# The start of a two-layer diffusion backbone: the first norm's squares and shift modulation on TensorE, the context's scale modulation on VectorE

## The chip, the cores and the metric

The kernel runs on one core of a Trainium2 chip. The metric is the device time of one execution in microseconds. Of several runs the median is taken. One further execution was taken by the hardware profiler; its times are those of the profile. The engines are called as the profile calls them: PE is TensorE, DVE is VectorE, ACT is ScalarE, POOL is GpSimd, SP is the engine that issues the DMA transfers.

## What is computed

The model has 512 latent tokens and 256 context tokens of width 1024, and two layers. Each sub-layer first normalises its input and modulates it. The start of the program, which is where the change lies, is this part of the reference:

```python
m_lat = jnp.moveaxis((jax.nn.silu(c) @ mod_w[l] + mod_b[l]).reshape(b, N_MOD, 1, D_MODEL), 1, 0)
m_ctx = (jax.nn.silu(c_ctx) @ mod_w[l] + mod_b[l]).reshape(N_MOD, 1, 1, D_MODEL)

def rmsnorm(x, g):
    xf = x.astype(jnp.float32)
    y = xf * lax.rsqrt(jnp.mean(xf * xf, axis=-1, keepdims=True) + EPS)
    return (y * g.astype(jnp.float32)).astype(x.dtype)

def modulate(h, g, shift, scale):
    return rmsnorm(h, g) * (1 + scale) + shift

def ffn_sublayer(h, m, j, g_pre, g_post, w13, w2):
    a = modulate(h, g_pre, m[3 * j], m[3 * j + 1])
    return h + FFN_RES * m[3 * j + 2] * rmsnorm(swiglu(a, w13, w2), g_post)
```

So before the first matrix product can run, the mean square of every token is needed, and two of the nine modulation vectors: the shift and the scale, each a product of the activated conditioning vector (one for latent, one for context tokens) with a 1024 x 1024 block of `mod_w`. The rest of the two layers (attention in the first, a state-space scan in the second, four feed-forward sub-layers, and the other modulation vectors) is not touched by the change.

## The kernel before

Activations are held with the feature on the partition: `h` has eight k tiles of 128 features, each 128 x 512 (latent) or 128 x 256 (context). Every large product keeps float32 accuracy with three matmuls: weights and activations are split in a high and a low part, and `mm3` (L861 to L863) issues high x high, high weight x low activation, low weight x high activation. The high part is made on ACT, the low part on DVE.

`start` prepares the first feed-forward sub-layer and returns `feed`, which is called once for each k tile, here called steps 0 to 7. The order is written out by hand; no planner places this work. Each engine runs its own instructions in the order of the program, so what stands first in `start` and `feed` stands first in its engine's queue.

* The squares of the latent tokens: ACT squares each k tile (`sq_acc`, L892 and L898), DVE adds seven of them into a sum (L899), and `rstd_a` lets PE sum over partitions by four products with a column of ones (L873). DVE adds the epsilon (L875), POOL takes the power -1/2 (L876), and `rstd_b` spreads the result over the partitions on PE (L883); that spread tile, in PSUM, is called R below.
* The modulation: the block of `mod_w` is read transposed, 16 tiles of 128 outputs x 1024 inputs (half a megabyte each): `m0d8` to `m0d15` for the scale, `m0d0` to `m0d7` for the shift, in a ring of nine buffers. For latent tokens DVE makes one dot per tile (`dot`, L651: product with the broadcast conditioning vector `cb` and sum). For context tokens POOL multiplies the tile in place (`prod`, L523) and ACT sums it (`close`, L516); four such tiles may be pending. `gains` (L505, L506) and `shifts` (L511) add the bias.
* The normalised activations: DVE makes `tmp` (L552), ACT its high part `ahi` with the shift as bias (L555), DVE the low part `alo` (L556).
* The weights of the first three rows of the feed-forward part are split by `high` (L496, ACT) and `low` (L500, DVE), two per row (gate and up).

Between the steps PE runs the matmuls that have become possible: the first row from step 0, the second from step 1, the third from step 4, at most two k tiles of a row at a time until the last step. That makes 6, 18, 12, 12, 24, 24, 24 and 24 matmuls in steps 0 to 7, 144 in all, called the first block here. Step 0 also issues all later transfers on SP, in order: the modulation tiles, the weights of rows 1 and 2, then the context tokens; step 7 issues the first background tiles (`mw`) and weights, and squares the context tokens. After the block the outputs of the three rows leave PSUM (L1056 on ACT, L1059 on DVE) and the context's chain begins. The remaining modulation tiles are worked off by DVE during the later matmuls, for both kinds of tokens.

Of the kernel before, what the change touches and what calls it, by code (L numbers as in the profile page):

```python
# [10 lines left out]
F32 = mybir.dt.float32  # L11
F32R = mybir.dt.float32r
AF = mybir.ActivationFunctionType
ALU = mybir.AluOpType
PSUM = bass.MemoryType.PSUM

P = 128
D = 1024
KT = D // P
NL = 512  # L20
# [5 lines left out]
LAT, CTX = 0, 1  # L26
# [21 lines left out]
LZP = 0.3  # L48
SALT = None
TRACE = None  # L50
CTXD = ()
HI = (1, 1, 2, 3)
FROM = (0, 1, 4)
CATCH = 2
# [14 lines left out]
class Graph:  # L69
# [4 lines left out]
    LAT = 0.15  # L74
# [337 lines left out]
class Model:  # L412
# [40 lines left out]
    def start(self, a, l=0, s=0):  # L453


        nc, tc, io = self.nc, self.tc, self.io
        m0 = tc.alloc_tile_pool(name="m0", bufs=1)
        self.cb = [self.modp.tile([P, D], F32, name=f"cb{v}") for v in (LAT, CTX)]
        cf = self.pp.tile([P, 2, 2, 8], F32, name=f"coef{l}_{s}")
        self.coef[l, s] = cf  # L460
        self.bg_done.update(((0, 0), (0, 1)))
        mod, bias, held, wd, prods, ws = self.modc[0], self.vec("mod_b0"), [], {}, [], {}
        box = [{}, {}]

        def load_c(v):
            nc.sync.dma_start(out=self.cb[v], in_=io[("c", "c_ctx")[v]].partition_broadcast(P))

        def silu(v):
            nc.scalar.activation(self.cb[v], self.cb[v], AF.Silu)

        def load(m):
            for t in (8 + m, m):
                wd[t] = m0.tile([P, D], F32, tag="wd", name=f"m0d{t}", bufs=9)
                nc.sync.dma_start(out=wd[t], in_=io["mod_wT"][0, t])

        def weights(r):

            if r == 2:
                n = [x.rearrange("p k t -> p (k t)") for x in self.new_a(CTX)]
            for up in (0, 1):  # L480
                if r == 1:
                    raw = m0.tile([P, SLOT], F32, name=f"m0raw{up}")
                    hi, lo = [m0.tile([P, SLOT], F32R, name=f"m0{x}{up}") for x in ("whi", "wlo")]
                else:
                    raw = self.wp.tile([P, SLOT], F32, tag="raw", name=f"raw{self.uid()}", bufs=2)
                    if r == 0:
                        hi, lo = [self.wp.tile([P, SLOT], F32R, tag=x, name=f"{x}{self.uid()}", bufs=3)
                                  for x in ("whi", "wlo")]
                    else:
                        hi, lo = [x[:, up * SLOT:(up + 1) * SLOT] for x in n]  # L490
                nc.sync.dma_start(out=raw, in_=io["w13"][0, 0, r, up])
                ws[r, up] = raw, hi, lo

        def high(r, up):
            raw, hi, lo = ws[r, up]
            nc.scalar.activation(hi, raw, AF.Copy)  # L496

        def low(r, up):
            raw, hi, lo = ws[r, up]
            nc.vector.tensor_tensor(lo, raw, hi.bitcast(F32), op=ALU.subtract)  # L500

        def gains(v, m, n=1):

            sh, sc = slice(m, m + n), slice(8 + m, 8 + m + n)
            nc.vector.tensor_tensor(mod[:, v, sc], mod[:, v, sc], bias[:, sc], op=ALU.add)  # L505
            nc.vector.scalar_tensor_tensor(cf[:, v, 0, sh], mod[:, v, sc], 1.0, self.vec("npre00")[:, sh],  # L506
                                           op0=ALU.add, op1=ALU.mult)

        def shifts(v, m, n=1):
            sh = slice(m, m + n)  # L510
            nc.vector.tensor_tensor(mod[:, v, sh], mod[:, v, sh], bias[:, sh], op=ALU.add)  # L511

        def close(n):
            while len(prods) > n:
                t = prods.pop(0)
                nc.scalar.activation(wd[t], wd[t], AF.Copy, accum_out=mod[:, CTX, t:t + 1])  # L516

        def prod(t):

            if t in CTXD:  # L520
                self.mod_dot(wd[t], 0, t, CTX)
            else:
                nc.gpsimd.tensor_tensor(wd[t], wd[t], self.cb[CTX], op=ALU.mult)  # L523
                prods.append(t)

        def dot(t):
            self.mod_dot(wd[t], 0, t, LAT)

        self.load_h(LAT, 2)
        load_c(LAT)  # L530
        load(0)
        for t, name in ((self.vecs, "vecs"), (self.ident, "ident")):
            nc.sync.dma_start(out=t, in_=io[name])
        weights(0)
        load_c(CTX)
        load(1)
        for m in range(KT):
            self.sq_acc(self.h[LAT][:, m], NL, m, box[LAT], nc.vector)
        silu(LAT)
        dot(8)  # L540
        self.rstd_a(box[LAT]["S"], NL, box[LAT])
        dot(0)
        gains(LAT, 0)
        shifts(LAT, 0)
        self.rstd_b(NL, box[LAT])
        high(0, 0)
        a[LAT]["hi"], a[LAT]["lo"] = self.new_a(LAT)

        def pre(k):

            t = self.tmp()
            nc.vector.scalar_tensor_tensor(t, self.h[LAT][:, k], cf[:, LAT, 0, k:k + 1], box[LAT]["R"],  # L552
                                           op0=ALU.mult, op1=ALU.mult)
            hi, lo, sh = a[LAT]["hi"][:, k], a[LAT]["lo"][:, k], mod[:, LAT, k:k + 1]
            nc.scalar.activation(hi, t, AF.Identity, bias=sh)  # L555
            return lambda: nc.vector.scalar_tensor_tensor(lo, t, sh, hi.bitcast(F32), op0=ALU.add, op1=ALU.subtract)  # L556

        def feed(k):
            if k == 0:
                load(2)  # L560
                weights(1)
                for m in range(3, KT):
                    load(m)
                    if m == W2:
                        weights(2)
                self.load_h(CTX)
            rest = pre(k)
            if k == 0:
                high(0, 1)
                silu(CTX)  # L570
                for t in (8, 0):
                    prod(t)
                low(0, 0)
            elif k + 1 < KT:
                dot(9 + k)
            rest()
            if k == 0:
                low(0, 1)
                dot(9)
            if k + 1 < KT:  # L580
                gains(LAT, k + 1)
                dot(1 + k)
                shifts(LAT, k + 1)
                for t in (9 + k, 1 + k):
                    prod(t)
            for i in range(4):
                if HI[i] == k:
                    high(1 + i // 2, i % 2)
                    low(1 + i // 2, i % 2)
            close(4)  # L590
            if k == KT - 1:
                self.mw_load()
                self.prime()
                for m in range(KT):
                    self.sq_acc(self.h[CTX][:, m], NCX, m, box[CTX], nc.vector)

        def done():
            self.ahead = 4

        self.ahead, self.quiet = 1, True  # L600
        tag = ("chain", l, -1, CTX, 0)
        first = 144 * NL / 2400.0
        self.seq.defer(first + 0.1, tag, lambda: (gains(CTX, 0, KT), shifts(CTX, 0, KT)))
        self.chain_pre(CTX, 0, NCX, l, s, box[CTX], first + T0C, tag, a[CTX])
        return feed, lambda: (close(0), m0.release()), done, ws

    def vec(self, name):
# [257 lines left out]
    def rstd_a(self, S, n, box, inv=1.0 / D):  # L865

        nc = self.nc
        nb = n // P
        ps = self.sbank()
        for b in range(nb):  # L870
            at = [b * P, 256 + b * P] if n <= 256 and inv == 1.0 / D else [b * P]
            for c in at:
                nc.tensor.matmul(ps[:, b:b + 1], S[:, c:c + P], self.ones[:, 0:1], start=c == at[0], stop=c == at[-1])  # L873
        r = self.tp.tile([P, 8], F32, tag="r", name=f"r{self.uid()}", bufs=4)
        nc.vector.tensor_scalar(r[:, :nb], ps[:, :nb], inv, EPS, op0=ALU.mult, op1=ALU.add)  # L875
        nc.gpsimd.tensor_tensor(r[:, :nb], r[:, :nb], self.mhalf[:, :nb], op=ALU.pow)  # L876
        box["r"] = r
# [1914 lines left out]
def layout(inputs):  # L2792

    a = {k: np.asarray(v) for k, v in inputs.items()}
    c = np.ascontiguousarray
    o = {}
# [11 lines left out]
    for l in range(2):  # L2808
        put(f"mod_b{l}", col(a["mod_b"][l]))
        for s in range(3):  # L2810
# [3 lines left out]
    put("kvn", col(a["mla_kv_norm"][0]))  # L2814
    put("sink", np.broadcast_to(a["swa_sink"][0][None, :], (P, 8)))
    o["vecs"] = vecs
    o["w13"] = c(a["ffn_w13"].reshape(2, 2, KT, P, 2, NFF, P).transpose(0, 1, 5, 4, 3, 2, 6)
                 .reshape(2, 2, NFF, 2, P, KT * P))
    o["w2"] = c(a["ffn_w2"].reshape(2, 2, NFF, P, KT, P).transpose(0, 1, 4, 3, 2, 5).reshape(2, 2, KT, P, NFF * P))
# [35 lines left out]
def tile_kernel(ctx, tc, io, stop=None):  # L2855
    m = Model(ctx, tc, io, stop)
    with tc.manual_schedule():
        m.build()


_IO = ["xT", "cT", "c", "c_ctx", "mod_wT", "vecs", "w13", "w2", "ident", "cst", "kcs", "csq", "w_in", "w_u", "w_out",
       "s5v", "s5d", "s5bc", "w_in5", "w_glu"]


# [18 lines left out]
```

## Time and profile before

| | us |
|---|---|
| median of 3 runs (2973.9 to 2978.47) | 2974.22 |
| the profiled execution | 2978.33 |
| its span, first to last instruction | 2976.5 |
| PE busy | 2825.5 (95%) |
| DVE busy | 1837.2 (62%) |
| ACT busy | 1039.1 (35%) |
| POOL busy | 777.4 (26%) |

Times in the profile's rows are microseconds from the start of the span unless marked ns. A row of the timeline gives start, duration, engine, line, operation, the tile written and those read, shapes, the number of instructions, and in brackets how long the engine was idle before and who released it. Matmul ends are modelled and overlap the next start, so spacing is read from start to start. A product of float32 operands that are not marked `fp32r` stands in the trace as two records. DVE's sums with an accumulator have a short second record. The mean granted TensorE clock of the execution is 0.973 of full speed.

### The profile page before, as it was taken

What the parts mean: (1) busy time and instruction counts of PE and PEld (TensorE: products, weight loads), DVE (VectorE), ACT (ScalarE), POOL (GpSimd) and SP (SyncE); (2) the same over time, 40 slices, a digit from 0 to 9 for tenths busy, and PEclk for the clock granted to TensorE, in tenths of its full rate; (3) what the DMA queues carried; (4) which work ended last, traced back from release to release, by engine and by line L of the source; (5) the groups of instructions that cost most, each with busy time, mean ns of one, the idle gap of its engine ahead of it and who ended that gap; (6) DMA issues with size and microseconds to landing.
All of it is one profiled execution on the core that took longest, in us unless ns stands there. A gap on an engine that the chain in (4) does not pass through costs nothing. (4 is left out here: it accounts for less than half of the span.)

```text
span 2976.5 us, 42015 instructions
## 1 busy us (share of the span) xinstructions
PE 2825.5 (95%) x16008; PEld 2445.7 (82%) x16008; DVE 1837.2 (62%) x3285; ACT 1039.1 (35%) x1813; POOL 777.4 (26%) x1239
## 2 busy tenths in 40 slices
PE   4999999989999989999999899999998999899997
PEld 3888888877788779888888788888887887888886
DVE  8788998684688587443544852543637694643334
ACT  3422121243677552222223422212224453432222
POOL 4100000151454240244244534244245000300001
PEclk7999999999899999999999999999999999999998
DMA  6365657633000232323233333232323562332332
GB/s 246 109 220 188 215 192 251 200 108 108 1 31 15 100 98 85 97 73 104 80 97 105 96 102 95 79 97 77 97 87 98 186 220 91 100 106 91 97 105 70
DMA packets 140809, 343.56 MB, mean 115 GB/s; under 512 B 13632, under 2 KB 61248, under 8 KB 138560
## 3 DMA queue, kind: packets, MB, share of 16 engines
q1 hardware_dynamic: 140608, 340.88, 35.5%
q8 instruction: 126, 2.06, 0.3%
q14 instruction: 75, 0.61, 0.1%
HBM read 311.53 MB, written 29.29 MB: 115 GB/s over the span
## 5 line engine op out<-in xcount | busy, mean ns | idle before, releaser
L861 PE MATMUL mm<-ahi,whi 128*128 128x512 f32 (+1 forms) x2128 | 740.6, 348 | 21.2 <-ACT ahi L555 16.7
L862 PE MATMUL mm<-alo,whi 128*128 128x512 f32 (+1 forms) x2128 | 735.7, 346 | 10.5 <-DVE alo L556 7.1
L863 PE MATMUL mm<-ahi,wlo 128*128 128x512 f32 (+1 forms) x2128 | 728.7, 342 | 4.6 <-DVE wlo L762 4.6
L762 DVE TENSOR_TENSOR wlo<-raw,whi 128x1024 fp32r<-128x1024 f32 (+2 forms) x391 | 452.5, 1159 | 380.9 <-ACT whi L752 363.0
L752 ACT ACTIVATE whi<-raw 128x1024 fp32r<-128x1024 f32 (+2 forms) x411 | 393.0, 957 | 302.6 <-PE mm L862 169.0
L861 PEld LDWEIGHTS mm<-ahi,whi 128*128 128x128 f32 x2128 | 407.0, 191 | 80.7 <-ACT ahi L555 18.8
L862 PEld LDWEIGHTS mm<-alo,whi 128*128 128x128 f32 x2128 | 406.8, 191 | 61.8 <-DVE alo L556 9.7
L863 PEld LDWEIGHTS mm<-ahi,wlo 128*128 128x128 f32 x2128 | 405.5, 191 | 55.5 <-DVE wlo L762 5.5
L861 PE MATMUL mm<-gh,whi 128*128 128x512 f32 x992 | 349.3, 352 | 0.9 <-ACT gh L910 0.8
L862 PE MATMUL mm<-gl,whi 128*128 128x512 f32 x992 | 348.5, 351 | 0.4 <-DVE gl L913 0.2
L863 PE MATMUL mm<-gh,wlo 128*128 128x512 f32 x992 | 345.9, 349 | 0.0
L899 POOL TENSOR_TENSOR S<-S,tmp 128x512 f32<-128x512 f32 (+1 forms) x25 | 27.3, 1092 | 1072.8 <-ACT tmp L898 1072.3
L651 DVE SCALAR_TENSOR_TENSOR mj<-mw,cb 128x1024 bf16<-128x1024 f32 x224 | 273.7, 1222 | 16.2 <-DMA mw<-in_mod_wT_dram 11.9
L910 ACT ACTIVATE gh<-tmp 128x512 fp32r<-128x512 f32 (+1 forms) x135 | 73.7, 546 | 531.5 <-DVE tmp L1059 530.5
L861 PEld LDWEIGHTS mm<-gh,whi 128*128 128x128 f32 x992 | 187.7, 189 | 30.0 <-issue 1.8
L862 PEld LDWEIGHTS mm<-gl,whi 128*128 128x128 f32 x992 | 187.4, 189 | 25.6 <-DVE gl L913 1.3
L863 PEld LDWEIGHTS mm<-gh,wlo 128*128 128x128 f32 x992 | 187.0, 188 | 26.1
L2163 POOL TENSOR_TENSOR s5t<-s5pw,s5bb 128x256 f32<-128x256 f32 x128 | 86.6, 704 | 442.1 <-PE mm L2174 354.8
L1059 DVE TENSOR_TENSOR tmp<-tmp,mm 128x512 f32<-128x512 f32 (+1 forms) x135 | 77.6, 575 | 188.6 <-PE mm L863 188.6
L1056 ACT ACTIVATE tmp<-mm 128x512 f32<-128x512 f32 (+1 forms) x135 | 63.2, 508 | 316.0 <-PE mm L863 316.0
L279 POOL TENSOR_TENSOR S<-S,tmp 128x256 f32<-128x256 f32 (+3 forms) x116 | 134.6, 1162 | 139.3 <-ACT tmp L276 132.6
L1100 DVE TENSOR_TENSOR y<-mm,y 128x512 f32<-128x512 f32 (+1 forms) x128 | 71.1, 586 | 111.2 <-PE mm L863 111.1
(460 smaller groups left out, 5021.3 us busy)
## 6 DMA issues: line engine op xcount, KB each, us to landing
raw<-in_w_dram SPq DMA_DIRECT2D x210, 512.0 KB, 3.8
mw<-in_mod_wT_dram SPq DMA_DIRECT2D x128, 512.0 KB, 3.9
raw<-in_w_dram SPq DMA_DIRECT2D x88, 384.0 KB, 3.1
raw<-in_w_dram SPq DMA_DIRECT2D x64, 320.0 KB, 3.0
raw<-in_w_in_dram SPq DMA_DIRECT2D x23, 512.0 KB, 3.5
m0d<-in_mod_wT_dram SPq DMA_DIRECT2D x16, 512.0 KB, 8.0
raw<-in_w_out_dram SPq DMA_DIRECT2D x16, 512.0 KB, 3.3
s5v<-s5v SPq DMA_DIRECT2D x64, 128.0 KB, 3.1
```

The lines of the kernel that those rows point to most:

```text
L279: add = lambda e: lambda: e.tensor_tensor(S(), S(), q["t"][:, :n], op=ALU.add)
L651: self.nc.vector.scalar_tensor_tensor(junk, w, 1.0, self.cb[v], op0=ALU.mult, op1=ALU.mult, accum_out=self.modc[l][:, v, t:t + 1])
L752: self.nc.scalar.activation(hi[:, :n], raw[:, :n], AF.Copy)
L762: (eng or self.nc.vector).tensor_tensor(lo[:, :n], raw[:, :n], hi[:, :n].bitcast(F32), op=ALU.subtract)
L861: mm(out, whi, xhi, start=first, stop=False)
L862: mm(out, whi, xlo, start=False, stop=False)
L863: mm(out, wlo, xhi, start=False, stop=last)
L910: nc.scalar.activation(hi, src, AF.Copy)
L1056: nc.scalar.activation(st["s", jj, q][:, :n], bk[g][:, cs], AF.Silu)
L1059: nc.vector.tensor_tensor(t[:, :n], t[:, :n], bk[g][:, cs], op=ALU.mult)
L1100: nc.vector.tensor_tensor(y, bk[g][:, :n_], y, op=ALU.add)
L2163: g_.tensor_tensor(o, x, y, op=ALU.mult)
```

## The change

Three things change in `start`, and nothing outside but two host-side arrays and a split of `rstd_a`.

1. The squares: ACT squares every k tile into a `tmp` tile, and PE sums each at once over the partitions: four products with the column of ones per k tile, 32 in all, accumulated in one PSUM bank. DVE's seven additions go. `rstd_r` is the second half of `rstd_a`.
2. The shift: its block of `mod_w` is read untransposed (`mod_w0`, the same eight tiles of half a megabyte) and is the stationary operand on PE; the moving operand is `ccol`, the two conditioning vectors as two columns, a new transfer of 8 KB that stands first in SP's queue and is activated by ACT first of all. Eight products per tile give 128 shifts for latent and context tokens together; `shift_out` (DVE) adds the bias to both. `shift(0)` and `shift(1)` stand before step 0 on PE, `shift(k + 2)` before the matmuls of step k.
3. The context's scale: `CTXD` now names tiles 8 to 15, so that `prod` makes a second dot on DVE instead of the product on POOL and the sum on ACT. The context's shift comes out of item 2, so POOL has no modulation left, and `close` finds nothing to sum.

```diff
-CTXD = ()
+CTXD = tuple(range(8, 16))
...
+        box, sums = [{}, {}], {}
+        ccol = self.modp.tile([P, KT, 2], F32, name="ccol")
+        nc.sync.dma_start(out=ccol, in_=io["ccol"])
...
-                nc.sync.dma_start(out=wd[t], in_=io["mod_wT"][0, t])
+                nc.sync.dma_start(out=wd[t], in_=io["mod_wT"][0, t] if t >= 8 else io["mod_w0"][t])
...
-        def shifts(v, m, n=1):
-            sh = slice(m, m + n)
-            nc.vector.tensor_tensor(mod[:, v, sh], mod[:, v, sh], bias[:, sh], op=ALU.add)
+        def shift(m):
+
+            if m == 0:
+                sums["sh"] = self.sbank()
+            for k in range(KT) if m < KT else ():
+                nc.tensor.matmul(sums["sh"][:, 2 * m:2 * m + 2], wd[m][:, k * P:(k + 1) * P], ccol[:, k], start=m == k == 0,
+                                 stop=k == KT - 1, skip_group_check=True)
+
+        def shift_out(m):
+            nc.vector.tensor_scalar(mod[:, :, m], sums["sh"][:, 2 * m:2 * m + 2], bias[:, m:m + 1], None, op0=ALU.add)
...
+        nc.scalar.activation(ccol, ccol, AF.Silu)
+        sq = self.sbank()
         for m in range(KT):
-            self.sq_acc(self.h[LAT][:, m], NL, m, box[LAT], nc.vector)
+            q = self.tmp()
+            nc.scalar.activation(q, self.h[LAT][:, m], AF.Square)
+            for b in range(NL // P):
+                nc.tensor.matmul(sq[:, b:b + 1], q[:, b * P:(b + 1) * P], self.ones[:, 0:1], start=m == b == 0,
+                                 stop=m == KT - 1, skip_group_check=True)
         silu(LAT)
+        shift(0)
         dot(8)
-        self.rstd_a(box[LAT]["S"], NL, box[LAT])
-        dot(0)
+        self.rstd_r(sq, NL, box[LAT], 1.0 / D)
         gains(LAT, 0)
-        shifts(LAT, 0)
+        shift_out(0)
         self.rstd_b(NL, box[LAT])
+        shift(1)
         high(0, 0)
...
                 silu(CTX)
-                for t in (8, 0):
-                    prod(t)
                 low(0, 0)
...
                 dot(9)
+                prod(8)
             if k + 1 < KT:
                 gains(LAT, k + 1)
-                dot(1 + k)
-                shifts(LAT, k + 1)
-                for t in (9 + k, 1 + k):
-                    prod(t)
+                shift(k + 2)
+                shift_out(k + 1)
+                prod(9 + k)
...
-        self.seq.defer(first + 0.1, tag, lambda: (gains(CTX, 0, KT), shifts(CTX, 0, KT)))
+        self.seq.defer(first + 0.1, tag, lambda: gains(CTX, 0, KT))
```

More of the change, by code (lines that the diff above doesn't have):

```diff
@@ L462, in start @@
         mod, bias, held, wd, prods, ws = self.modc[0], self.vec("mod_b0"), [], {}, [], {}
-        box = [{}, {}]
+        box, sums = [{}, {}], {}
+        ccol = self.modp.tile([P, KT, 2], F32, name="ccol")
+        nc.sync.dma_start(out=ccol, in_=io["ccol"])
         def load_c(v):
@@ L873, in rstd_a, with rstd_r @@
                 nc.tensor.matmul(ps[:, b:b + 1], S[:, c:c + P], self.ones[:, 0:1], start=c == at[0], stop=c == at[-1])
+        self.rstd_r(ps, n, box, inv)
+    def rstd_r(self, ps, n, box, inv):
+        nc, nb = self.nc, n // P
         r = self.tp.tile([P, 8], F32, tag="r", name=f"r{self.uid()}", bufs=4)
@@ L2816, in layout @@
     o["vecs"] = vecs
+    o["mod_w0"] = c(a["mod_w"][0][:, :D].reshape(KT, P, KT, P).transpose(2, 1, 0, 3).reshape(KT, P, D))
+    o["ccol"] = c(np.stack([a["c"][0].reshape(KT, P).T, a["c_ctx"].reshape(KT, P).T], axis=2))
     o["w13"] = c(a["ffn_w13"].reshape(2, 2, KT, P, 2, NFF, P).transpose(0, 1, 5, 4, 3, 2, 6)
@@ L2858, in tile_kernel @@
         m.build()
-_IO = ["xT", "cT", "c", "c_ctx", "mod_wT", "vecs", "w13", "w2", "ident", "cst", "kcs", "csq", "w_in", "w_u", "w_out",
+_IO = ["xT", "cT", "c", "c_ctx", "ccol", "mod_w0", "mod_wT", "vecs", "w13", "w2", "ident", "cst", "kcs", "csq", "w_in", "w_u", "w_out",
        "s5v", "s5d", "s5bc", "w_in5", "w_glu"]
```

## The prediction

> **What bounds the kernel now.** I read the page first, for the whole span.
>
> ```profile
> PE   4999999989999989999999899999998999899997
> PEclk7999999999899999999999999999999999999998
> ```
>
> TensorE is full in every slice of 74 us but the first. What the first slice wins should therefore reach the end undiminished, and nothing else is worth looking for. Next comes the table of busy time by stage. The stages are cut where the first norm's modulating instruction (L552) starts for each k tile, so a row is one step of the loop that feeds the first matmuls; the last two rows are step 7 and what follows. The columns are PE, PEld, DVE, ACT and POOL busy with counts, granted clock, DMA share and GB/s.
>
> ```profile
> 18.31:31.08 12.77, 3.30 (x6) 1.78 (x6) 12.67 (x11) 2.62 (x3) 8.06 (x4) 0.83 0.94 385
> 31.08:43.31 12.23, 5.15 (x10) 3.29 (x11) 12.16 (x12) 4.70 (x7) 7.49 (x3) 0.50 0.28 86
> ...
> 60.31:68.06 7.75, 4.39 (x11) 3.10 (x11) 7.68 (x11) 2.80 (x5) 5.05 (x2) 0.74 0.61 206
> ...
> 83.85:92.37 8.52, 8.52 (x38) 6.98 (x36) 5.88 (x10) 7.74 (x17) 2.41 (x1) 0.95 0.05 6
> 92.37:120.00 27.63, 24.32 (x132) 20.58 (x131) 18.99 (x35) 14.31 (x25) 0.70 (x1) 0.94 0.32 97
> ```
>
> In each step DVE is busy 99% and PE about half. From 83.85 on PE is full. So up to there the pace is DVE's, and the list of waits of the first 120 us says the same: PE waits for `ahi`, and ACT's `ahi` waits for DVE's `tmp`.
>
> ```profile
> ACT ahi L555 <- DVE tmp L552: 45.6, 8, 10.1
> PE mm L861 <- ACT ahi L555: 16.7, 4, 9.2
> ```
>
> Third, the order of instructions inside step 4, on DVE and then on POOL.
>
> ```profile
> 60.31 0.74 DVE L552 SCALAR_TENSOR_TENSOR tmp<-h,coef,st 128x512 f32<-128x512 f32 x1
> 60.96 2.72 DVE L651 SCALAR_TENSOR_TENSOR mj<-m0d,cb 128x1024 bf16<-128x1024 f32 x1
> ...
> 63.62 0.74 DVE L556 SCALAR_TENSOR_TENSOR alo<-tmp,modc,ahi 128x512 fp32r<-128x512 f32 x1
> 64.28 2.33 DVE L505 TENSOR_TENSOR modc<-modc,vecs 128x1 f32<-128x1 f32 x1
> 66.64 0.16 DVE L506 SCALAR_TENSOR_TENSOR coef<-modc,vecs 128x1 f32<-128x1 f32 x1
> 66.72 1.22 DVE L651 SCALAR_TENSOR_TENSOR mj<-m0d,cb 128x1024 bf16<-128x1024 f32 x1
> ...
> 67.98 0.16 DVE L511 TENSOR_TENSOR modc<-modc,vecs 128x1 f32<-128x1 f32 x1
> ```
> ```profile
> 63.83 2.76 POOL L523 TENSOR_TENSOR m0d<-m0d,cb 128x1024 f32<-128x1024 f32 x1 [1.23 <-DVE mj L651]
> ```
>
> Adding one column takes 2.33 us beside a POOL product, the dot 2.72 us instead of 1.22. The groups by line give the free and the held duration of the same instruction (min, median, max in ns):
>
> ```profile
> L505 DVE TENSOR_TENSOR modc<-modc,vecs x9: 154/2333/2349, 15.2 to 101.2; 128x1 f32<-128x1 f32 x8, 128x8 f32<-128x8 f32 x1
> L500 DVE TENSOR_TENSOR alo<-raw,ahi x2: 1224/2307/3390, 49.6 to 59.2; 128x1024 fp32r<-128x1024 f32 x2
> ```
>
> So almost half of a DVE step is time in which POOL's multiplications hold DVE up.
>
> **The change part by part.**
>
> *POOL and ACT lose the context's modulation.* Sixteen POOL products and sixteen ACT sums go. DVE exchanges eight latent shift dots for eight context scale dots of the same size, and the shift's addition (0.16) for `shift_out`, for which I take the same 0.16. So DVE's count stays and only the holding goes. Free costs, start to start in the rows above: L552 0.66, dot with its read 1.25, L556 0.66, gains about 0.25, shift 0.1, a `low` 1.15 (estimated from 1.22 less the overlap of some 0.07 between neighbours). Step 0: 0.66 + 2 x 1.15 + 0.66 + 3 x 1.25 + 0.35 = 7.7 instead of 12.77. Step 1: 0.66 + 2 x 1.25 + 0.66 + 0.35 + 2 x 1.15 = 6.5 instead of 12.23. Steps 2 and 3, with one `low`: 5.3. Steps 4 to 6: 4.2 instead of 7.75.
>
> *The squares move to PE.* Seven DVE additions go, 32 products against a column of ones come. Prices, and what they replace:
>
> ```profile
> 11.72 1.78 PEld L873 LDWEIGHTS st<-ones,S 128*128 128x128 f32 x8 [11.72 <-DVE S L899]
> 14.15 1.99 POOL L876 TENSOR_TENSOR r<-r,mhalf 128x4 f32<-128x4 f32 x1 [13.27 <-DVE r L875]
> 16.19 2.08 PE L883 MATMUL st<-ident,r 128*128 128x128 f32 x8 [2.60 <-POOL r L876]
> ```
> ```profile
> 737.71 1.39 PE L873 MATMUL st<-ones,S 128*128 128x1 f32 x12
> 738.97 0.49 PE L861 MATMUL mm<-ahi,whi 128*128 128x512 f32 x1
> ```
>
> Eight records are four products: 0.445 us each at the start, and 1.26 / 6 = 0.21 at full clock. [...] If the two columns of a shift cost twice the price, each shift would be 1.7 us dearer and the sum below 7 us later.
>
> All 32 cold: 14.2 us. They begin near 5.6 (first square, plus 0.5 for the new `ccol` transfer at the head of SP's queue). The clock opens on a grid of 3.41 us, read off the changes of matmul duration:
>
> ```profile
> 54.02:57.43 3.41, 2.73 (x6) 1.84 (x7) 3.41 (x4) 3.39 (x6) 2.58 (x1) 0.50 0.02 8
> 57.43:60.84 3.41, 3.12 (x8) 1.92 (x6) 3.34 (x7) 0.00 (x0) 1.93 (x2) 0.50 0.90 277
> 60.84:64.25 3.41, 0.50 (x1) 0.19 (x1) 3.41 (x4) 2.80 (x5) 2.18 (x2) 1.00 0.19 40
> 64.25:67.66 3.41, 3.25 (x8) 2.57 (x9) 3.38 (x4) 0.00 (x0) 2.34 (x1) 0.50 0.95 332
> ```
>
> A window that was 91% busy is followed by full clock, one at 15% by half, one at 80% by half. With one or two cold windows (to 9.0 or 12.4) the squares end at 14.1 or 15.9; I take 15. Then `r` 0.2, POOL's power 2.0 with `shift(0)` (eight products, 1.7) beside it, and the spreading products, about 1.2 at full clock: 18.4, against 18.31, where step 0 starts now. Bounds: 17.5 if the power is faster without a DVE dot beside it, 25.5 if all of it runs at half clock (19.8, shift 3.6, spreading 2.1). A table load more or less on ACT, whose first function is now `Silu` on `ccol`, moves `dot(8)` and not R: DVE has nothing else to do until the squares end. Without that cover it would cost its 1.3 us.
>
> *PE gets the shifts.* Seven more groups of eight products, 1.7 us each at full clock, 3.6 at half. PE's queue runs in order, so `shift(k+2)` stands before step k's matmuls. While DVE sets the pace, PE's idle half covers it; afterwards each costs its price. The matmuls: 144 in the eight steps (6, 18, 12, 12, then 24 each), at
>
> ```profile
> 87.15 0.39 PE L861 MATMUL mm<-ahi,whi 128*128 128x512 f32 x1
> ...
> 92.60 0.95 PE L873 MATMUL st<-ones,S 128*128 128x1 f32 x8
> ```
>
> 5.45 us for 24 of them, 0.227 each, and at half clock
>
> ```profile
> 65.01 0.63 PE L863 MATMUL mm<-ahi,wlo 128*128 128x512 f32 x1
> ...
> 67.14 0.63 PE L862 MATMUL mm<-alo,m0whi 128*128 128x512 f32 x1
> ```
>
> 2.13 us for 5, 0.427 each.
>
> *The transfers.* The number of half-megabyte tiles stays, and so does the ring of nine.
>
> ```profile
> m0d<-in_mod_wT_dram SPq DMA_DIRECT2D x16, 512.0 KB, 8.0
> 10.45 3.33 SPq L474 DMA_DIRECT2D m0d<-in_mod_wT_dram  x4
> 15.99 1.58 SPq L474 DMA_DIRECT2D m0d<-in_mod_wT_dram  x2
> 22.43 40.77 SPq L474 DMA_DIRECT2D m0d<-in_mod_wT_dram  x8
> ```
>
> The third shift tile, issued last of the four, lands near 13.4 + 8.0 = 21.4, the fourth near 25.6: PE waits for them, but steps 0 and 1 are held longer by DVE (below). The last eight issues crawl today because a buffer is freed only after POOL and ACT. Now a shift tile is free after its eight products and a scale tile after the second dot: `m0d7` waits for step 2's end (37.9) and lands by 46 to 48, needed near 55. That slack of 7 us also covers what stands behind it on SP, the context stream and the next weights.
>
> *The sum.* With R at 18.4 DVE starts the steps at 18.4, 26.1, 32.6, 37.9, 43.2, 47.4, 51.6 and 55.8, and `alo` follows 2.6 later (0.66 + 1.25 + 0.66). PE is last held by the second `low` of step 1, at 32.6. Left then are 9 matmuls of step 1 (2.0), four shifts (6.7), steps 2 and 3 (5.4) and steps 4 to 7 (96 x 0.227 = 21.8): 36.0 us at full clock. DVE stays just ahead (`alo` of step 4 at 45.8, PE there at 47). One and a half windows at half clock before it warms cost half of 5.1: 2.6. So the first block ends at 32.6 + 36.0 + 2.6 = 71.2 instead of 92.6: **21.4 us less**. Behind it one more wait goes:
>
> ```profile
> 92.83 0.58 ACT L1056 ACTIVATE tmp<-mm 128x512 f32<-128x512 f32 x1
> 94.39 0.50 PE L861 MATMUL mm<-ahi,whi 128*128 128x512 f32 x1 [0.84 <-DVE tmp L1059]
> ```
>
> The last four of ACT's sums ran to 92.8 and held the first output back; they are gone, and the bank of the first row is complete 4 us before the block's end. That is 0.8; 0.4 of it is given back for the `ccol` issue. 21.8 in all. What is late next is the context's chain between 92 and 120, 3.3 us of idle PE today; it isn't touched. The profiled run took 2978.3 (span 2976.5), 4.1 above the median of 2974.2. It should become 2956.5, and the median 2952.4, which I round up to **2953**, since a part of the 4.1 may lie in the very stage that goes.
>
> **The rivals.**
>
> *Half clock to step 3* (2962). Matmuls in small groups between waits may keep PE falling back: the work from 32.6 to step 4 is 12.4 us at full and 24.7 at half clock, 12.3 more, of which 2.6 is counted: gain 12. For it: the windows above alternate. Against it: they do so because PE idles, and work that doubles leaves no idle. [...]
>
> *Late start* (2960). R at 25.5: every DVE step moves 7.1, PE's hold with it, gain 21.8 - 7.1 = 15.
>
> *DVE isn't relieved* (2973). If the long instructions were held by something other than POOL, say transfers, equal counts on DVE leave 0.8 to win. Against it: the 2.33 falls in 63.83 to 66.59, POOL's row, and without a POOL product the same add takes 0.154 (the minimum in its group).
>
> *PE becomes the bound at half clock* (2983, slower). Mechanism: products of one or two columns are nearly all weight loading; if that doesn't count as work for the clock, each shift closes it again for the matmuls behind. Place: from R at 25.5 to the block's end. Price: seven shifts and 144 matmuls are 11.8 + 32.7 = 44.5 at full, 24.9 + 61.5 = 86.4 at half clock. It ends at 92.6, no gain, when 54% of that is done at half clock; at three quarters it ends at 101.4, 8.8 later. For it: nothing in the trace has eight such products before each group. Against it: a window that held four of them (0.95 at 92.60), busy 75% with and 47% without them, was followed by full clock:
>
> ```profile
> 91.53:94.94 3.41, 2.57 (x16) 2.22 (x15) 0.75 (x2) 2.40 (x6) 0.70 (x1) 1.00 0.48 154
> 94.94:98.35 3.41, 3.41 (x19) 2.84 (x17) 2.49 (x4) 1.72 (x4) 0.00 (x0) 1.00 0.00 0
> ```
>
> *More* (2948). R at 17.5 and a warm clock from the start: 31.7 + 36.0 = 67.7.
>
> **How the numbers follow.** The forecast, 2948.5 to 2957, gets 0.70; half clock 0.12; late start 0.07; more 0.02; no relief 0.04; slower 0.05. 0.2% is 5.9 us, about what this kernel's runs can tell from nothing. Faster: 0.70 + 0.12 + 0.07 + 0.02 = 0.91; same 0.04; slower 0.05. The range goes from below the best case, 2946, to above half clock, 2964.
>
> **What would show it.** Right: L505 at 0.16 throughout; POOL empty between the power and the context's; the eight L552 at about 18, 26, 33, 38, 43 and then some 4 to 5 apart; PE over 90% busy from 33; the first block's end near 71; PE's idle time after it as before. The step on the squares is right if their 64 records end by 16 with the later ones at 0.11 spacing. Wrong: R beyond 20, a step of DVE above 6 after step 1 while PE waits, PE waiting for a `m0d` transfer after 30, or a granted clock of 0.50 in the stage from 37 on.

## The result, and the profile after

The median fell from 2974.22 to **2959.63 us** (2955.48 to 2966.83 in 7 runs): a ratio of 0.9948, with a 95% interval of 0.9934 to 0.9961. The kernel before lay at 2971.95 to 2978.47 in the 7 runs beside it, so the two sets do not overlap. The gain of the medians is 14.6 us; 21.2 was forecast. The profiled execution of the changed kernel took 2966.83 us (its span 2965.1), 11.5 less than the profiled one of before.

The page of the changed kernel, its slices of PE and of the granted clock:

```profile
PE   9999999989999989999999899999998999899997
PEclk9999999998799999999999999999999999999998
```

The first slice is full now, as the others were. What is missing of the gain has to be looked for inside that slice. Behind it the tenth and eleventh slice (667 to 815 us) show a clock of 0.8 and 0.7, where it was 0.9 and 0.8. I return to both.

PE's records in the first block of the changed kernel (start, us, engine, line, operation, tiles, shapes, count; in brackets the idle time before and what ended it). L552 are the squares, L516 the shifts, L901 the spreading products, L887 the first work behind the block:

```profile
5.57 13.82 PE L552 MATMUL st<-ones,tmp 128*128 128x1 f32 x64 [5.57 <-ACT tmp L550]
19.25 3.55 PE L516 MATMUL st<-ccol,m0d 128*128 128x2 f32 x16
22.66 2.06 PE L901 MATMUL st<-ident,r 128*128 128x128 f32 x8
24.50 6.83 PE L516 MATMUL st<-ccol,m0d 128*128 128x2 f32 x32
33.90 3.41 PE L516 MATMUL st<-ccol,m0d 128*128 128x2 f32 x16
44.02 1.84 PE L516 MATMUL st<-ccol,m0d 128*128 128x2 f32 x16
81.17 0.95 PE L887 MATMUL st<-ones,S 128*128 128x1 f32 x8
```

The block ends at 81.17 instead of 92.60. The squares take 13.8 us without a gap, 0.215 us a record: their spacing is the same at the end as at the start, and twice that of the record at full clock (0.106, from the 1.70 us for 16 records at 44.02). The first four shifts take 3.4 us each, the next one 1.7 (from 44.02 to 45.72, where the next step's matmuls start). The busy times by stage of the changed kernel (PE, PEld, DVE, ACT, POOL busy, granted clock, DMA share, GB/s), from the squares to behind the block:

```profile
5.57:19.30 13.73, 13.73 (x65) 13.73 (x65) 1.23 (x2) 6.02 (x9) 0.00 (x0) 1.00 1.04 402
24.50:31.19 6.69, 6.69 (x33) 6.69 (x33) 6.29 (x10) 2.62 (x3) 0.00 (x0) 1.00 0.78 265
37.16:45.72 8.56, 8.56 (x35) 7.08 (x36) 6.33 (x11) 1.67 (x2) 0.00 (x0) 1.00 1.01 368
50.29:55.22 4.93, 4.78 (x30) 4.03 (x30) 4.89 (x9) 1.20 (x2) 0.00 (x0) 1.00 0.28 95
55.22:64.70 9.48, 9.12 (x42) 7.46 (x42) 4.99 (x14) 0.72 (x1) 0.00 (x0) 0.82 0.09 38
75.73:81.17 5.44, 5.44 (x25) 4.51 (x24) 1.65 (x3) 0.60 (x1) 0.00 (x0) 1.00 0.31 99
81.17:109.00 27.83, 25.23 (x145) 22.04 (x144) 20.13 (x35) 14.72 (x24) 0.70 (x1) 0.94 0.28 95
```

From 24.50 to 81.17 PE is idle for 0.5 us in all (0.15 in the row from 50.29, 0.36 in the row from 55.22), and in most rows DVE is not full: the bound has gone over from DVE to PE, also in the early steps. Only in step 3 (the row from 50.29) are both nearly full. The clock column reads 1.00 in the first rows although the records there stand at twice the spacing of full clock. So at the start of this program the spacing of the records is to be read, not that column. The list of PE's records shows the real opening, at 42.8 us, inside step 1:

```profile
42.43 0.59 PE L875 MATMUL mm<-ahi,m0whi 128*128 128x512 f32 x1
42.86 0.40 PE L876 MATMUL mm<-alo,m0whi 128*128 128x512 f32 x1
```

On DVE, the group of the one-column add (min, median, max in ns by the line of the changed kernel) is at its short duration throughout, and POOL's column in the rows above is empty up to 81.17:

```profile
L507 DVE TENSOR_TENSOR modc<-modc,vecs x9: 151/155/160, 19.5 to 89.7; 128x1 f32<-128x1 f32 x8, 128x8 f32<-128x8 f32 x1
```

### The profile page after: what moved, and what is told of

It is laid out like the page before. It is cut to its first block, busy times and chain, and to the rows that moved or that the text cites. A ratio compares the mean times of both kernels' runs of the same rounds, so it can differ in the third digit from the quotient of the medians.

```text
span 2965.1 us, 42324 instructions
## 1 busy us (share of the span) xinstructions
PE 2849.9 (96%) x16192; PEld 2475.4 (83%) x16192; DVE 1803.5 (61%) x3277; ACT 1020.7 (34%) x1781; POOL 735.8 (25%) x1223
```

## The experiments

Two theories stood after the result. **A, the clock**: products with one or two moving columns do not open PE's clock, so squares and early shifts run at half clock, R comes 6 us late, and PE binds from there. **B, the exchange**: what is won is only DVE's relief from POOL, and what is lost is PE work in itself, whatever the clock. A third question was which part of the change brings what. As the block's end is a mark that scatters little (between two profiles of one kernel by 0.04 us for the changed kernel and 0.85 us for the one with both wide, below), and the time scatters by several us, each result gives both: the time against the kernel before on the same chip, and the start of the row that corresponds to 81.17 above.

### The squares back on DVE

```diff
 for m in range(KT):
-    q = self.tmp()
-    nc.scalar.activation(q, self.h[LAT][:, m], AF.Square)
-    for b in range(NL // P):
-        nc.tensor.matmul(sq[:, b:b + 1], q[:, b * P:(b + 1) * P], self.ones[:, 0:1], ...)
+    self.sq_acc(self.h[LAT][:, m], NL, m, box[LAT], nc.vector)
...
-shift(0)
 dot(8)
-self.rstd_r(sq, NL, box[LAT], 1.0 / D)
+self.rstd_a(box[LAT]["S"], NL, box[LAT])
+shift(0)
```

> The changed kernel with its squares back on DVE (seven additions, then four products); shift and context scale as changed. Theory: the 32 one-column products run at half clock throughout (13.8 us in the profile after) and make R late, and PE, which is then the bound, hands that on. Then R comes at 19 to 20 instead of 24.7, the first block ends near 76 instead of 81.2, and the time is 2954 to 2956 against 2959.6 for the change. Rival: the squares cost nothing since PE has work waiting for transfers anyway; then the block still ends near 81 and the time stays within 2 us of the change.

2960.7 us, ratio 0.994 (0.9921 to 0.9959). PE's records of this kernel:

```profile
17.83 2.05 PE L896 MATMUL st<-ident,r 128*128 128x128 f32 x8
20.82 6.96 PE L516 MATMUL st<-ccol,m0d 128*128 128x2 f32 x32 [0.94 <-DMA m0d<-in_mod_w_dram]
77.54 0.95 PE L882 MATMUL st<-ones,S 128*128 128x1 f32 x8
```

The steps start 4.8 us earlier than in the changed kernel (the spreading products at 17.83 against 22.66), and the block ends 3.6 earlier. So this half of the change lengthens the block as it stands. In the medians those 3.6 us can't be seen, 2960.7 against 2959.63, and the time that was expected, 2954 to 2956, did not come.

### The squares with 128 columns, then the shifts with 64

```diff
-nc.tensor.matmul(sq[:, b:b + 1], q[:, b * P:(b + 1) * P], self.ones[:, 0:1], ...)
+nc.tensor.matmul(sq[:, b * P:(b + 1) * P], q[:, b * P:(b + 1) * P], self.ones, ...)
```

and in the second kernel also

```diff
-nc.tensor.matmul(sums["sh"][:, 2 * m:2 * m + 2], wd[m][:, k * P:(k + 1) * P], ccol[:, k], ...)
+nc.tensor.matmul(sums["sh"][:, 64 * m:64 * m + 64], wd[m][:, k * P:(k + 1) * P],
+                 cwide[:, k].rearrange("p a b -> p (a b)"), ...)
```

The extra columns are copies; as many products are issued, with more work in each. One column of each copy is read afterwards, and ACT writes the copies of the two conditioning columns.

> The changed kernel with 128 moving columns of ones instead of one in the 32 products of the squares: the same weight loads and the same sums, only more columns of result. Theory: a product of one or two columns does not count as work for the clock, one of 128 does. Then the records go from 0.21 to about 0.11 us after one or two windows (9 to 12.4 us), the squares end at 14 to 16, R at 18 to 19.5, the time is 2953 to 2956. Rival: the slow products come from something else at the start of the program, such as the transfers into the same memory; then the records stay at 0.21 or grow, R stays at 24.7 or later, and the time is 2959 to 2962.

> As the one before, and the shift products with 64 moving columns too (the two conditioning columns repeated 32 times by ACT). Theory of the clock: squares and shifts both hold it open, a shift costs 1.7 us instead of 3.4 before 43 us and no cold window follows in steps 3 to 5; R at 18 to 19.5, the first block ends at 68 to 71, as first predicted, and the time is 2948 to 2952. If 64 columns are too few to count, it equals the one before, 2953 to 2956. Rival (not the clock): 2959 or more.

2959.13 us, 0.9939 (0.992 to 0.9957), and 2960.2 us, 0.994 (0.9921 to 0.9959). PE's records of the kernel with wide squares:

```profile
5.54 9.90 PE L552 MATMUL st<-ones,tmp 128*128 128x128 f32 x64 [5.54 <-ACT tmp L550]
15.28 1.84 PE L516 MATMUL st<-ccol,m0d 128*128 128x2 f32 x16
20.06 6.07 PE L516 MATMUL st<-ccol,m0d 128*128 128x2 f32 x32 [1.94 <-DVE wlo L502]
28.80 3.54 PE L516 MATMUL st<-ccol,m0d 128*128 128x2 f32 x16
76.33 0.95 PE L887 MATMUL st<-ones,S 128*128 128x1 f32 x8
```

and of the one with both wide:

```profile
20.49 6.09 PE L517 MATMUL st<-cwide,m0d 128*128 128x64 f32 x32 [2.01 <-DVE wlo L503]
29.49 1.97 PE L517 MATMUL st<-cwide,m0d 128*128 128x64 f32 x16 [0.53 <-DMA m0d<-in_mod_w_dram]
36.91 1.89 PE L517 MATMUL st<-cwide,m0d 128*128 128x64 f32 x16
72.50 0.95 PE L889 MATMUL st<-ones,S 128*128 128x1 f32 x8
```

The same 64 records with 128 times the columns take 9.9 us instead of 13.8, and the first two-column shift behind them runs at full clock (1.7 us, from 15.28 to 16.98). Then PE stands idle for 1.94 and 2.01 us (the profile names DVE's `wlo` here, and the transfer of `m0d` in a second profile of the kernel with both wide), and in both kernels the granted clock falls to 0.50, at 21.0 and 21.7 us. The next two shifts are slow in both, with two columns (6.07 us for the pair) and with 64 (6.09). The difference comes after that: with 64 columns the clock is open again at 28.5 us, and the shift at 29.49 takes 1.97 us; with two columns it opens at 38.1, and the shift at 28.80 takes 3.54. The transfers, the rival named before the run, went on beside the wide squares at 375 to 412 GB/s, against 402 over the squares of the changed kernel. Theory A holds: the block ends 4.8 and 8.7 us earlier (76.33 and 72.50 against 81.17), with more arithmetic on PE, which B excludes. Only their median times do not follow: 0.5 us less and 0.6 more than the changed kernel. Both were expected lower, 2953 to 2956 and 2948 to 2952.

### The number of columns that opens the clock

The wide squares with 32 columns, `self.ones[:, 0:32]`.

> As the kernel with 128 columns in the squares alone, with 32 columns. If what counts for the clock is how long the array streams, 32 columns (a quarter) may be too few: the squares then run at 0.21 us a record to about 19 as with one column. If any result wider than a few columns counts, they end at 15 to 16 as with 128.

A single run: 2963.54 us. The squares and the block's end on PE in this kernel:

```profile
5.56 13.86 PE L552 MATMUL st<-ones,tmp 128*128 128x32 f32 x64 [5.56 <-ACT tmp L550]
81.26 0.95 PE L887 MATMUL st<-ones,S 128*128 128x1 f32 x8
```

13.86 us, as with one column, and the block ends as in the changed kernel. So 32 columns left the closed clock closed here, and 128 columns (9.9 us) did not. 64 columns are not settled: in the kernel with both wide PE did nothing but 64-column products from 21.7 to 26.3 us, and the clock opened only at 28.5, behind 2 us of matmuls with 512 columns.

### Each half of the change alone, on the kernel before

The squares alone (the change's loop and `rstd_r`, nothing else), and, in a second kernel, all products of the modulation on DVE with neither PE part, by one constant:

```diff
-CTXD = ()
+CTXD = tuple(range(16))
```

> The kernel before with one part of the change alone: the squares summed by 32 one-column products on PE instead of seven additions on DVE; all modulation as before. Theory: these products run at half clock to about 19.3, R comes at 23 to 24.5 instead of 18.3, and since DVE, held by POOL, sets the pace of the steps, all of that is handed on: the first block ends near 98 instead of 92.6 and the time is 3 to 6 us above the kernel before. Rival: freeing DVE of the additions is worth as much as the products cost: within 2 us of before.

> The kernel before with one constant changed: all sixteen context products of the start on DVE, none on POOL or ACT; squares and latent modulation as before, nothing on PE. DVE then makes four dots in each step instead of two. Theory that POOL's products hold DVE up: free of them a step is 0.66 + 4 x 1.25 + 0.66 + 0.35 = 6.7 us against 7.8 now, steps 0 to 3 about 10, 9, 8 and 8 against 12.8, 12.2, 9.6 and 7.4; the block ends near 80 to 83, and the time is 2962 to 2966, nearly all of the change's gain without PE. Rival: the long instructions have another cause; then sixteen more dots of 1.25 make the block end near 112 and the time about 2994.

The squares alone are **slower**: 2984.46 us, 1.002 (1.0005 to 1.0034). In that kernel the spreading products start 4.8 us later than before (16.19) and the block ends 4.4 later:

```profile
4.87 13.81 PE L542 MATMUL st<-ones,tmp 128*128 128x1 f32 x64 [4.87 <-ACT tmp L540]
20.97 2.08 PE L892 MATMUL st<-ident,r 128*128 128x128 f32 x8 [2.28 <-POOL r L885]
97.00 0.95 PE L878 MATMUL st<-ones,S 128*128 128x1 f32 x8
```

All products on DVE: 2973.64 us, 0.9969 (0.9952 to 0.9986). DVE's and PE's records of that kernel:

```profile
62.16 0.74 DVE L552 SCALAR_TENSOR_TENSOR tmp<-h,coef,st 128x512 f32<-128x512 f32 x1
68.64 0.74 DVE L552 SCALAR_TENSOR_TENSOR tmp<-h,coef,st 128x512 f32<-128x512 f32 x1
```
```profile
82.81 0.95 PE L873 MATMUL st<-ones,S 128*128 128x1 f32 x8
```

A DVE step with four dots takes 6.48 us (68.64 - 62.16) without POOL beside it, where step 4 of the kernel before took 7.75 with two dots and POOL; the block ends 9.8 us earlier. Taking POOL's multiplications away is thus worth nearly as much of the block as the whole change (11.4), without one product on PE. The time is less clear: 2962 to 2966 was expected, the 12 runs scatter from 2955.13 to 2975.82, and their mean lies 8.3 us below that of the kernel before on the same chip, the median only 3.2.

### The context's scale products back on POOL

The changed kernel with `CTXD = ()`: eight products go back to POOL and ACT.

> The changed kernel with the context's scale products back on POOL and ACT (eight instead of the sixteen of before). Theory: after the change PE, not DVE, is the bound from R on, so DVE may be held again without loss: steps of 5 to 8 us on DVE still end before PE, block end near 81, time within 2 us of 2959.6. Rival: the gain of the change comes from freeing DVE of POOL in every step; then the instructions beside POOL take 2.3 instead of 0.16 again and the time rises by 4 us or more, to 2964 or above.

2965.8 us, 0.9961 (0.9945 to 0.9976). From the groups of DVE, and from PE's records, of this kernel:

```profile
L507 DVE TENSOR_TENSOR modc<-modc,vecs x9: 159/2319/2357, 19.4 to 90.1; 128x1 f32<-128x1 f32 x8, 128x8 f32<-128x8 f32 x1
```
```profile
81.53 0.95 PE L887 MATMUL st<-ones,S 128*128 128x1 f32 x8
```

DVE is held again at 2.32 us an add, but the block ends only 0.36 us later: with PE as the bound, DVE's relief in this part is covered. So the block's end is where the theory put it, and the time is where the rival put it. The mean of its 12 runs is 3.8 us above that of the changed kernel's 13 runs (2965.1 against 2961.3), with a 95% interval of -0.8 to 8.4; 0.36 of it is in the block, and whether the rest is more than scatter is not settled.

### What is left: the order of the shifts, and two of them on DVE

On the kernel with both wide, the shift of step k+1 is issued ahead of step k, not that of k+2, and then also shifts 6 and 7 are computed as dots on DVE, from tiles read transposed:

```diff
-shift(1)
...
+if k + 1 < KT:
+    shift(k + 1)
...
-    shift(k + 2)
```
```diff
+if m >= 6:
+    self.mod_dot(wd[m], 0, m, LAT)
+    self.mod_dot(wd[m], 0, m, CTX)
+    nc.vector.tensor_scalar(mod[:, :, m], mod[:, :, m], bias[:, m:m + 1], None, op0=ALU.add)
```

> The kernel with 128 and 64 columns, and each group of shift products one step later: shift(k+1) stands before the matmuls of step k, where shift(k+2) stood. In the profiles DVE's shift_out(k+1) waits until shift(k+2), which writes the same PSUM bank, has ended (1.6 us in step 0 and 0.8 in step 1 of the kernel with wide columns, 1.9 to 4.6 in the change). Theory: the wait goes, PE does one group of products less before step 0, and the first block ends at 69 to 70 instead of 72; mean time 2953 to 2957. Rival: PE has as much to do as before and DVE's waits were free; block end 71.5 to 73, no difference.

> The kernel before this one with the last two shifts (6 and 7) back on DVE as dots, two for each, from the transposed block: PE loses 32 of its 64 late records' groups (two groups of 1.75 us), DVE gains 2.5 us in each of steps 5 and 6, where it waits for PE. Theory that PE alone is the bound in steps 4 to 7: block end 66 to 68, mean time 2950 to 2955. Rival: DVE becomes the bound in steps 5 to 7; block end 69 to 71, no gain.

2959.77 us, 0.9938 (0.9919 to 0.9958), and **2955.75 us** (2946.98 to 2959.22), 0.9919 (0.9897 to 0.9941), the lowest of all. The ends of their blocks:

```profile
70.97 0.95 PE L889 MATMUL st<-ones,S 128*128 128x1 f32 x8
```
```profile
67.55 0.95 PE L894 MATMUL st<-ones,S 128*128 128x1 f32 x8
```

The order is worth 1.5 us of the block, or 0.7 against a second profile of the kernel it was made from (71.65). It was meant to take away DVE's waits in `shift_out`, and it did not. From the lists of waits of the first 110 us, of the kernel with both wide and of the reordered one:

```profile
DVE modc L522 <- PE st L517: 7.8, 5, 3.1
DVE modc L522 <- PE st L517: 8.7, 5, 3.2
```

`shift_out` now waits for its own shift, which comes later. The expected block end (69 to 70) and time (2953 to 2957) were both missed. Two shifts fewer on PE (3.4 us at 1.7) are worth 3.42. By its median the last version beats the kernel before by 25.0 us on its chip and lies below the changed kernel; its interval overlaps the changed kernel's, so by how much it is better is not settled. Block end and mean time (2954.1) came as expected, 66 to 68 and 2950 to 2955.

### Does the block's gain reach the end?

The changed kernel and the one with both wide once more, on another chip.

> The changed kernel unchanged, beside the next one on the same chip. In six profiles the time behind the first block ran from 2876 to 2889 us, and went with the half-clock time in it. If that is chance from run to run, the means of this and the next differ by what their first blocks differ, 8.7 us (81.2 against 72.5); if the rest gives the gain back, they stay within 3 us.

> The kernel with 128 columns in the squares and 64 in the shifts, unchanged. First block again near 72. If the gain of the block reaches the end: mean 2951 to 2956 and 6 to 10 us below the one before. If it is given back later: 2958 to 2962, within 3 us of it.

2963.94 us, 0.9941 (0.9919 to 0.9963), and 2956.8 us, 0.993 (0.9912 to 0.9948). On this chip the means are 4.2 us apart (95% interval -2.9 to 11.4), between the two cases expected. Over both sets, which are not from one chip, they are 2961.3 (13 runs) and 2958.4 (12 runs): 3.0 us apart, with a 95% interval of -1.1 to 7.0, where the blocks differ by some 9. So for this pair the block's gain does not seem to arrive in full, but the runs on one chip alone do not show it. Over the ten kernels with several runs a straight line, weighted by the number of runs, through mean time against block end (67.55 to 97.00) has a slope of 1.0 us per us, with single kernels up to 4.4 us off it. So the gain arrives on the whole, and a deviation of a few us belongs to the single kernel.

Where the deviation lies can be seen, not why it comes. From the block's end to the first transposes of the attention every profile takes 669 to 675 us. Behind that, by stages from 760 to 780 us (columns as above), for the kernel before (with a second row from 788), the changed one, and the one with both wide:

```profile
760.00:780.00 20.00, 18.80 (x115) 15.39 (x114) 13.93 (x41) 13.97 (x42) 8.42 (x8) 1.00 0.01 1
788.00:805.00 17.00, 17.00 (x65) 14.58 (x64) 10.55 (x29) 9.00 (x27) 6.78 (x8) 0.50 0.00 0
```
```profile
760.00:780.00 20.00, 19.51 (x71) 15.73 (x71) 12.72 (x36) 11.35 (x36) 8.73 (x9) 0.58 0.00 0
```
```profile
760.00:780.00 20.00, 20.00 (x73) 16.09 (x71) 12.29 (x34) 9.98 (x31) 7.87 (x9) 0.51 0.00 1
```

These 20 us don't hold the same instructions in the three, but the clock is 0.51 to 0.58 in two of them although PE is 98 and 100% busy there, and 1.00 in the one where it is 94% busy. The kernel before has its closed stretch later, the 17 us from 788 to 805. Such a stretch lies between 755 and 805 us in every one of these profiles, but it is not equally long: 24 us in the changed kernel, 24 and 17 in two profiles of the kernel with both wide, and 3.5 in that with the context's products back on POOL, whose time behind the block is the shortest of the six. Over the profiles of six kernels the time behind the block goes with the time at half clock there (104 to 148 us, summed from the granted clock), 0.27 us for each. What closes the clock at that place, and for how long, was not tried.

## Why the prediction was right or wrong

**Right: DVE was held by POOL.** The rival that something else held it falls: the add is at 0.155 us throughout, it is at 2.32 us again when eight products go back to POOL, and in the kernel with all products on DVE a step of four dots takes 6.48 us, where the prediction's free prices make 0.66 + 4 x 1.25 + 0.66 + 0.35 = 6.7.

**Right: the two prices of a shift.** 1.7 us at full clock (44.02 to 45.72), and 3.4 at half where 3.6 was taken; the second column cost nothing (0.426 us a product with two columns, 3.41 / 8, and 0.432 with one, 13.82 / 32, both at half clock). The trace also agrees that the 32 products are 64 records.

**Right: the transfers.** PE waits for no `m0d` after 30 in the changed kernel. Such waits begin to show between 20 and 30 us when PE is faster (0.53 us at 29.49 with both wide, 3.0 at 20.24 in the reordered kernel).

**Wrong: "With one or two cold windows the squares end at 14.1 or 15.9; I take 15."** The step assumed that a window full of one-column products opens the clock. 13.7 us of them, the length of four windows, did not. The squares end at 19.3, R is 24.7 (22.66 + 2.06) and not 18.4. It is what *late start* named, at 25.5, and it fits what the rival on the *slower* side supposed, that such products don't count as work for the clock. The argument against that rival was a window with four such products among sixteen records, busy 75%, followed by full clock; half of that window's 16 records were others, so the row told nothing of a window of narrow ones alone. And the clock reads 1.00 in that window already, so the row showed a clock that stayed open and not one that opened. By the rows above, 13.8 us of back-to-back records with 1 or 32 moving columns did not open it, while with 128 columns the same records sped up on the way (9.9 us).

**Wrong: "While DVE sets the pace, PE's idle half covers it."** The rows showed PE 26% busy in step 0 and 57% in step 4, at a pace that DVE set. In the changed kernel PE has no idle half from R on, since it runs at half clock until 42.8. The block's work from 24.50 to 81.17 took 56.7 us, of which PE idled 0.5 (0.36 of it in the stage from 55.22 to 64.70); by the prediction's own prices it is 44.5 at full and 86.4 at half clock. The surplus of 11.7 is the half-clock stretch 24.5 to 42.8 (half of 18.3 is 9.2), one half-clock window in step 4 (1.7 of 3.41), and 0.8 that I don't assign. That window can be seen in the granted clock, behind a shift at 53.52:

```profile
56.45:59.85 3.40, 3.40 (x10) 2.65 (x9) 3.40 (x6) 0.72 (x1) 0.00 (x0) 0.51 0.00 0
```

The rival *slower* needed 54% of the way from full to half clock to lose the whole gain; here it was 11.7 of 41.9, 28%. So the sum was 71.2 for the block's end and the measurement 81.17: 6.3 for the late R, and the remaining 3.7 for the colder steps. Of the signs of being wrong that were named, two came: R beyond 20, and a granted clock near 0.50 behind 37.

**Not foreseen: `shift_out(k+1)` waits for `shift(k+2)`.** All shifts write one PSUM tile, and on DVE the reading of column pair k+1 waits until the products for the next pair, issued ahead of it, are done. From the list of waits of the first 120 us, and DVE's longest one, of the changed kernel:

```profile
DVE modc L520 <- PE st L516: 11.6, 4, 4.6
```
```profile
64.88 0.23 DVE L520 TENSOR_SCALAR modc<-st,vecs 128x2 f32<-128x2 f32 x1 [4.61 <-PE st L516]
```

11.6 us of DVE waiting. That it is off the path is argued from PE, which is busy meanwhile. The reordered kernel above does not test it, since DVE's waits for the shifts stayed (8.7 us).

**Wrong: "That is 0.8", from the first output's bank.** ACT's sums are gone and PE's wait stayed, as PE's and DVE's records of the changed kernel show:

```profile
82.96 0.50 PE L875 MATMUL mm<-ahi,whi 128*128 128x512 f32 x1 [0.85 <-DVE tmp L1077]
```
```profile
82.15 0.16 DVE L893 TENSOR_SCALAR r<-st 128x2 f32<-128x2 f32 x1 [4.67 <-PE st L887]
82.23 0.68 DVE L1077 TENSOR_TENSOR tmp<-tmp,mm 128x512 f32<-128x512 f32 x1
```

DVE's sum of the first output stands behind the context's `r` in DVE's queue, and `r` waits for the products at 81.17. What ended last was not the bank but the order on DVE. This term should have been zero.

**The first sentence held:** what the first slice wins reaches the end. In the profiled pair the time from the block's end to the span's end is 2883.9 us in both (2976.5 - 92.60 and 2965.1 - 81.17). Not counted was that it scatters by more than 10 us from profile to profile (2876.3 to 2888.9 in the profiles of six kernels). The direction and the range came true, and the median lies at the time of *late start*, 2960; the likeliest case, 2948.5 to 2957, did not come. That the median fits *late start* so well is in part luck: that rival has R late and the clock warm, which would end the block at 78.3 (71.2 + 7.1), and it took 81.17. The block gained 11.4 us and so did the profiled execution (11.5), while the medians differ by 14.6.

## What to carry to other kernels

Before small products are moved to PE at the start of a program, look at how many columns they move: in these runs, from a closed clock, products with one or 32 columns ran on at half clock even back to back (13.8 and 13.9 us for the squares), shifts with two columns took 3.4 us each, and 128 columns of copies made the records of the squares faster (9.9 us). With the clock already open, two-column products ran at full speed (1.7 us a shift from 44.02 on). Count an engine's new work at both clocks and in its queue's order; where work is taken off one engine, ask whether removing the one that holds it (here POOL, 9.8 us of the block) isn't most of the gain. Check on the trace that an edit meant to remove a wait has removed it. Judge a part of a few us by a mark close behind it, here the block's end, since the time of the whole scatters by more than the part.

## What the runs showed of the hardware

A float32 product with 128 x 128 weights cost 0.43 us at half clock whether it moved 1, 2 or 32 columns (13.82 / 32, 3.41 / 8, 13.86 / 32). Making it wider made it cheaper at the start of this program: the 64 records of the squares took 13.8 us with one column and 9.9 with 128. In the changed kernel the granted clock read 1.00 over records that ran at half speed, up to the first opening at 42.8 us. And a stage of the attention ran for 20 us at a clock of 0.51 with PE busy all the time (760 to 780 us, in the kernel with both wide); how long that stretch was differed from profile to profile (3.5 to 24 us).
